# Encoder layer on one core: the long sequence's first phase with other rooms, earlier norms, a later fourth transposition and a held order

## The chip, the cores and the metric

One Trainium2 chip, one core of it. The metric is the device time of one execution in microseconds (us), median over the runs shown. The core's engines run beside each other and wait for each other through semaphores: TensorE (matmuls and transpositions), VectorE, ScalarE, GpSimd, and the queues that start DMA transfers (here mostly SyncE's, called the load queue below). Each engine takes its own instructions strictly in the order in which they stand in its stream.

## The reference

One hybrid encoder layer, run on two sequences with the same weights: the short one of 512 tokens (`x_sample`) and the long one of 1024 (`x_prompt`), model width 1024.

```python
def _trunk(x, ...):
    h = x
    h = h + _token_mixer(_rmsnorm(h, norm_mix_g), w_in, ...)
    h = h + jnp.square(jax.nn.relu(_rmsnorm(h, norm_mlp_g) @ w_mlp_up)) @ w_mlp_down
    return _rmsnorm(h, norm_final_g)

def _token_mixer(xn, w_in, ...):
    z = xn @ w_in
    qa, ka, va, qb, kb, vb, ga, gb = jnp.split(z, idx, axis=-1)
    qa = _apply_rope(_rmsnorm(qa per head, q_norm_g), cos, sin)
    ka = _apply_rope(_rmsnorm(ka per head, k_norm_g), cos, sin)
    o_a = _gqa_attention(qa, ka, va)
    o_b = _neighbourhood_attention(qb, kb, vb, rpb)
    merged = sigmoid(ga) * (o_a @ w_proj_a) + sigmoid(gb) * (o_b @ w_proj_b)
    return merged @ w_out
```

Branch A has 8 query heads in two groups, each with one key and one value head of 64. `_rmsnorm` divides by the root mean square of a row and multiplies by a gain.

## The kernel before

Every matmul of the mixer keeps about fp32 precision by splitting each operand into a high part (rounded by a ScalarE copy) and a low part (the difference, by VectorE), and by three products, high x high, high x low and low x high (`mm3`, L161 to L163). So each operand costs a ScalarE copy and a VectorE subtraction on its way to TensorE, for weights (`split`, L150 and L156) as for activations.

The two sequences run one after the other (`run`), then the MLP of both. Inside a sequence come the phases R (projections of branch A for one head group, twice), A (attention), B (neighbourhood attention) and G (gates, output projection, the norm for the MLP). Where the short sequence ends, its phase G already norms the first four 128-row tiles of the long one: for each of its own four tiles it loads a tile `xa` of the long sequence, norms it (`norm_tile`, tile `xnns`), and one tile later transposes it on TensorE and splits it into the long sequence's operands `xs_0h` and `xs_0l` (`p0_t` and `transpose_tile`, L241, L251, L255). `ahead` holds what waits to be transposed. The fourth is transposed after the loop.

The change lies in the long sequence's first phase R, group 0. Its loop goes over eight tiles `tt`. In each it:

- transposes tile `tt + 1` if phase G did not, and norms tile `tt + 2` (`p0`); tile 4 is normed at the end of `tt == 1` (`norm_to`, L232 and L234);
- loads the rotary rows `rt` (L537), and projects tile `tt` to queries, keys and the branch-A value (`zs`, 24 matmuls of 384 columns);
- from the third tile on, computes branch B's values of tile `tt - 2` (`values`: `zvs`, 24 matmuls of 256 columns, evicted to `vts`, L522 and L523) and transposes the normed heads of tile `tt - 2` (`heads_t`, L496 to L505);
- norms the heads of tile `tt`, the head norm below: five squares with sums on ScalarE (L561), one scaling on VectorE (`ms_As`, L144), a power of -1/2 on GpSimd (`rs_As`, L146), five products on VectorE (`ts`, L565), the value head's high copy and low part (`vhls`, L568 and L569), two products for the rotation on GpSimd (`us`, L577), then a product and a sum on VectorE (L583, `rrs` L585).

A tile norm of 1024 columns is a square with sum on ScalarE (L223 or L232), a scaling on VectorE, a power on GpSimd and a product on VectorE (L227 or L234). It is the same sequence as a head norm, with one row sum.

Order. The program is written in one order, and a planner at build time lays out each engine's stream: whatever its own timing says is ready, earliest in program order first. An instruction can therefore stand in the stream ahead of others that were written before it. `tc.keep_in_program_order(op)` pins an instruction behind the one that was written just before it on its engine. It adds no wait on the chip, it fixes the place in the stream. A run of instructions that are all pinned keeps exactly the written order; what isn't pinned may still come between them.

Rooms. A pool of a phase gives each tag (`xt`, `xn`, `rt`, `sq` and so on) its own rooms, side by side in the order in which the tags first ask. With `reuse_waits="tile"` a tile of a phase waits only for those tiles of the phase before that lay on the same bytes. Phase G's pool, from its bottom, in KB: 0 to 16 four rooms `k4` (loaded tiles `xa`, normed tiles `xnhs` and `xnns`), 16 to 28 six rooms for residual rows, 28 to 32 and 32 to 36 two gain rows, 36 to 52 two rooms of the output weights' second half. Phase R lies over it, before the change: loaded tiles `xt` 0 to 8, normed tiles `xn` 8 to 16, value weights 16 to 32, gain row 32 to 36, and from 36 on, over the output weights, `rt`, `sq`, `t`, `u`, `rr`, `vt`.

Accumulators are four banks tagged `mm` (projections and values) and two double banks tagged `big` (transpositions of tiles and heads). Longer-lived operands are in slots of 8 KB, six on the left, eleven on the right.

Of the kernel before, what the change touches and what calls it, by code (L numbers as in the profile page):

```python
# [18 lines left out]
P = 128  # L19
D = 1024  # L20
# [41 lines left out]
def encoder(ctx: ExitStack, tc: tile.TileContext, xs, outs, w):  # L62
# [79 lines left out]
    def rstd(ss, n, width, name):  # L142
        m = sml.tile([P, 8], F32, tag="ms", name=f"ms_{name}")
        nc.vector.tensor_scalar(m[:, :n], ss, 1.0 / width, EPS, op0=ALU.mult, op1=ALU.add)  # L144
# [27 lines left out]
    def load_cols(src, off, ncol, name, alloc=None, pin=False, hold=None):  # L172
# [9 lines left out]
        for k0 in range(0, nk, kp):  # L182
# [16 lines left out]
            cut = partial(split, hi[:, kk : kk + kn, :], lo[:, kk : kk + kn, :], rv)  # L199
# [30 lines left out]
    def norm_to(xn, src, gb, nm):  # L230
        ss = sml.tile([P, 8], F32, tag="ss", name=f"ss{nm}")
        nc.scalar.activation(xn, src, AF.Square, accum_out=ss[:, 0:1])  # L232
        r = rstd(ss[:, 0:1], 1, D, nm)
        nc.vector.scalar_tensor_tensor(xn, src, r[:, 0:1], gb, op0=ALU.mult, op1=ALU.mult)  # L234
        return xn
# [79 lines left out]
    class Trunk:  # L315
        def __init__(self, sq, x, t0):
# [5 lines left out]
            self.ready = 0  # L322

# [6 lines left out]
        def p0_t(self, tt, xn):  # L330
# [3 lines left out]
            transpose_tile(xn, self.xhl[tb], j, f"x{self.N}_{tt}", self.t0 + tt == 0)  # L334
            self.ready = tt + 1
# [7 lines left out]
    def run(tr, nxt, first):  # L343
# [88 lines left out]
        def load_v(g, alloc, pin=False):  # L432
            return load_cols(win, 1792 + 256 * g, 256, f"v{N}_{g}", alloc, pin)

        early = {}
        for g in range(2):
            with phase(f"phR{N}_{g}") as ph:
                xn_of = {}
                fresh = g == 0 and tr.ready < NT
                if fresh and not first:  # L440

                    xt = norm_load(x, tr.ready, ph, f"{N}_{tr.ready}")
# [46 lines left out]
                rr_of = {}  # L489

                def heads_t(tt):
# [8 lines left out]
                    nc.scalar.activation(kT[:, 0, ts_], pt[:, 2, :], AF.Copy)  # L500
                    for e in range(2):
                        nc.scalar.activation(qT[e][half[e], :, ts_], pt[half[e], 0:2, :], AF.Copy)
                    nc.vector.tensor_tensor(kT[:, 1, ts_], pt[:, 2, :], kT[:, 0, ts_].bitcast(F32), op=ALU.subtract)
                    for e in range(2):
                        nc.vector.tensor_tensor(  # L505
                            qT[e][half[1 - e], :, ts_],
                            pt[half[e], 0:2, :],
                            qT[e][half[e], :, ts_].bitcast(F32),
# [432 lines left out]
        with phase(f"phG{N}") as ph:  # L941
# [155 lines left out]
            while ahead:  # L1097
                nxt.p0_t(*ahead.pop(0))
# [548 lines left out]
```

## Time and profile before

| | |
|---|---|
| median of 3 runs | 2178.33 us (2174.81 to 2178.46) |
| the profiled execution | 2175.84 us |
| its span, first to last instruction | 2174.1 us |
| mean granted TensorE clock | 0.997 |
| TensorE busy / VectorE / ScalarE / GpSimd | 98% / 67% / 51% / 16% |

The long sequence's first phase begins at 394.8 us of the span, with the first projection, and its last head transposition is at 472.1. In the lines of a timeline the columns are start, duration, engine, source line, operation, the tile written and the tiles read, the shape, the count, and in brackets how long the engine had been idle and which instruction ended that. Consecutive records of one engine overlap a little, because instructions are pipelined: the distance from start to start is what an instruction costs its engine. A waits view names the engine and line that waited, the instruction that released it, the sum in us, how often, and the longest.

### The profile page before, as it was taken

To read this page: it belongs to the slowest core of one execution; us is meant where nothing else is said; L and a number is where in the kernel's file an instruction comes from. 1 tells how busy PE (TensorE), PEld (TensorE's weight loads), DVE (VectorE), ACT (ScalarE), POOL (GpSimd) and SP (SyncE) were. 2 spreads that over 40 slices of the span, in tenths; PEclk is the share of its full clock that TensorE was granted. 3 is DMA by queue.
4 is the path that set the end of the run, shared out by engine and by line. 5 is a ranking of instruction groups with operands and counts; after the bars stand their busy time and mean duration, and the time that the engine had idled before them with its cause. 6 is when DMAs were issued, how large, how long until landed. Compare 5 with 4: busy or idle time off the path is not lost. (4 is left out here: it accounts for less than half of the span.)

```text
span 2174.1 us, 32424 instructions
## 1 busy us (share of the span) xinstructions
PE 2133.4 (98%) x11180; PEld 1867.9 (86%) x11180; DVE 1456.2 (67%) x2835; ACT 1109.9 (51%) x2377; POOL 350.4 (16%) x458
## 2 busy tenths in 40 slices
PE   8999999899999999999999999999999999999998
PEld 8888778888898888888888899998999988888886
DVE  6665566767757754555772777778777777769663
ACT  5654553556645744545531466656555643433452
POOL 2232210333233223322300200003000000000000
PEclk9999999999999999999999999999999999999999
DMA  6436447620123133423463656568554799788561
GB/s 183 137 103 179 136 143 250 206 78 28 44 72 89 40 90 93 123 76 115 134 194 136 207 177 198 175 227 224 159 156 151 233 347 347 221 269 289 175 197 65
DMA packets 319917, 351.48 MB, mean 162 GB/s; under 512 B 31368, under 2 KB 255240, under 8 KB 319752
## 3 DMA queue, kind: packets, MB, share of 16 engines
q1 hardware_dynamic: 278071, 280.17, 41.3%
q10 hardware_dynamic: 36000, 52.18, 6.9%
q0 software_dynamic: 5680, 17.04, 2.8%
q8 instruction: 89, 1.46, 0.3%
q14 instruction: 77, 0.62, 0.1%
HBM read 265.37 MB, written 87.88 MB: 162 GB/s over the span
## 5 line engine op out<-in xcount | busy, mean ns | idle before, releaser
L163 PE MATMUL dn<-wd,al 128*128 128x512 f32 x624 | 242.8, 389 | 0.0
L162 PE MATMUL dn<-wd,ah 128*128 128x512 f32 x624 | 242.8, 389 | 0.0
L161 PE MATMUL dn<-wd,ah 128*128 128x512 f32 x624 | 242.7, 389 | 0.0
L1124 ACT ACTIVATE ah<-ar 128x512 fp32r<-128x512 f32 x168 | 104.0, 627 | 198.7 <-PE dn L162 179.6
L1125 DVE TENSOR_TENSOR al<-ar,ah 128x512 fp32r<-128x512 f32 x168 | 115.4, 695 | 73.4 <-ACT ah L1124 66.7
L162 PEld LDWEIGHTS dn<-wd,ah 128*128 128x128 f32 x624 | 117.1, 188 | 24.5
L161 PEld LDWEIGHTS dn<-wd,ah 128*128 128x128 f32 x624 | 117.1, 188 | 24.3
L163 PEld LDWEIGHTS dn<-wd,al 128*128 128x128 f32 x624 | 117.1, 188 | 24.2
L668 DVE TENSOR_TENSOR ptls<-pTs,pths 128x512 fp32r<-128x512 f32 x160 | 107.8, 687 | 37.4 <-ACT pths L667 36.7
L667 ACT ACTIVATE pths<-pTs 128x512 fp32r<-128x512 f32 x160 | 94.3, 598 | 75.1 <-PE pTs L662 72.8
L628 POOL TENSOR_SCALAR ps<-ps,rls 128x1024 f32<-128x1024 f32 (+1 forms) x96 | 96.9, 1010 | 217.3 <-DVE rls L627 197.2
L622 DVE TENSOR_REDUCE nms<-ss 128x1 f32<-128x1024 f32 (+1 forms) x96 | 99.9, 1041 | 25.7 <-PE ss L620 25.2
L161 PE MATMUL gpss<-xs_0h,w_gs 128*128 128x512 f32 x256 | 106.0, 414 | 0.8 <-DVE rlbs L838 0.7
L625 ACT ACTIVATE ps<-ss,nms 128x1024 f32<-128x1024 f32 (+1 forms) x96 | 93.3, 973 | 22.9 <-DVE nms L622 20.0
L662 PEld LDWEIGHTS pTs<-ident,ps 128*128 128x128 f32 x640 | 78.2, 140 | 27.9 <-POOL ps L628 3.9
L163 PE MATMUL gpss<-xs_0h,w_gs 128*128 128x512 f32 x256 | 101.5, 397 | 0.2 <-DVE w_gs L156 0.2
L162 PE MATMUL gpss<-xs_0l,w_gs 128*128 128x512 f32 x256 | 101.4, 396 | 0.0
L662 PE MATMUL pTs<-ident,ps 128*128 128x128 f32 x640 | 98.8, 274 | 1.1 <-DVE ptls L668 0.3
L146 POOL TENSOR_TENSOR rs_f<-ms_f,mhalf 128x1 f32<-128x1 f32 x6 | 4.0, 667 | 590.7 <-DVE ms_f L144 590.7
L1124 ACT ACTIVATE A<-S 128x512 fp32r<-128x512 f32 x128 | 75.8, 623 | 30.8 <-DVE S L1187 23.5
L831 DVE CUSTOM_DVE_ANT_0 sbss<-sbs,bms 128x384 f32<-128x384 f32 (+1 forms) x96 | 48.6, 508 | 58.9 <-issue 34.1
L161 PE MATMUL ud<-B,A 128*128 128x384 f32 x256 | 85.7, 335 | 1.5 <-DVE c L1242 1.5
(316 smaller groups left out, 6439.2 us busy)
## 6 DMA issues: line engine op xcount, KB each, us to landing
ar<-ud SPq DMA_DIRECT2D x120, 512.0 KB
br<-in_w_mlp_down_dram SPq DMA_DIRECT2D x72, 512.0 KB
rawu<-in_w_mlp_up_dram SPq DMA_DIRECT2D x64, 512.0 KB
ud<-c ACTq DMA_DIRECT2D x128, 192.0 KB
raw_gs<-in_w_in_dram SPq DMA_DIRECT2D x32, 512.0 KB
zgs<-sgs ACTq DMA_DIRECT2D x48, 256.0 KB
ud<-cs SPq DMA_DIRECT2D x64, 192.0 KB
raw_os<-in_w_out_dram SPq DMA_DIRECT2D x16, 512.0 KB
```

The source lines that it names most:

```text
L161: nc.tensor.matmul(out, ah, bh, start=start, stop=False, **kw)
L162: nc.tensor.matmul(out, ah, bl, start=False, stop=False, **kw)
L163: nc.tensor.matmul(out, al, bh, start=False, stop=stop, **kw)
L622: nc.vector.tensor_reduce(nm_, s, axis=AX.X, op=ALU.max, negate=True)
L625: nc.scalar.activation(p, s, AF.Exp, bias=nm_, accum_out=l)
L628: nc.gpsimd.tensor_scalar(p, p, rl, 1.0, op0=ALU.mult, op1=ALU.mult)
L662: nc.tensor.transpose(pt[:, j * P : (j + 1) * P], PP[u, j][:, kc * P : (kc + 1) * P], ident)
L667: nc.scalar.activation(hi, pt, AF.Copy)
L668: nc.vector.tensor_tensor(lo, pt, hi.bitcast(F32), op=ALU.subtract)
L831: nc.vector.tensor_tensor_reduce(out=sb, in0=so, in1=bm, op0=ALU.add, op1=ALU.min, scale=-1.0, scalar=3e38, accum_out=nm_)
L1124: nc.scalar.activation(hi, src, AF.Copy)
L1125: nc.vector.tensor_tensor(lo, src, hi.bitcast(F32), op=ALU.subtract)
```

## The change

Four edits, all in or for that phase; the short sequence's own first phase keeps its code.

1. Rooms. The tags of the head norm (`vt`, `sq`, `rt`, `t`, `u`, `rr`) ask for their first room before everything else, in that order, then the gain row, `xt`, `xn` and the value weights. They then lie at 0 to 16.25 KB, 16.25 to 20.25, 20.25 to 28.25, 28.25 to 36.25 and 36.25 to 52.25. The load of the gain row is written before the load of the fifth tile.
2. Norms a tile sooner. Tile 5 is normed at the end of `tt == 2`, tile `tt + 3` at the start of `tt` from 3 on, where it was tile `tt + 2`. Tile 4 stays at the end of `tt == 1`.
3. The fourth tile. Its norm in phase G goes to a left slot instead of a `k4` room. It is carried over, and its transposition is written behind the head norm of the first tile in phase R.
4. Order held. In this phase the tile norms, the splits of transposed tiles from the fourth on, and all ScalarE and VectorE instructions of values, head transpositions and head norms are pinned. The GpSimd instructions, the matmuls, the transfers and the splits of weights are not.

The new arguments `hold` and `pin_split` of the weight loads are not used by a call.

```diff
-    def rstd(ss, n, width, name):
+    def rstd(ss, n, width, name, pin=False):
         m = sml.tile([P, 8], F32, tag="ms", name=f"ms_{name}")
-        nc.vector.tensor_scalar(m[:, :n], ss, 1.0 / width, EPS, op0=ALU.mult, op1=ALU.add)
+        op = nc.vector.tensor_scalar(m[:, :n], ss, 1.0 / width, EPS, op0=ALU.mult, op1=ALU.add)
+        if pin:
+            tc.keep_in_program_order(op)
...
-    def norm_to(xn, src, gb, nm):
+    def norm_to(xn, src, gb, nm, pin=False):
         ss = sml.tile([P, 8], F32, tag="ss", name=f"ss{nm}")
-        nc.scalar.activation(xn, src, AF.Square, accum_out=ss[:, 0:1])
-        r = rstd(ss[:, 0:1], 1, D, nm)
-        nc.vector.scalar_tensor_tensor(xn, src, r[:, 0:1], gb, op0=ALU.mult, op1=ALU.mult)
+        op = nc.scalar.activation(xn, src, AF.Square, accum_out=ss[:, 0:1])
+        if pin:
+            tc.keep_in_program_order(op)
+        r = rstd(ss[:, 0:1], 1, D, nm, pin)
+        op = nc.vector.scalar_tensor_tensor(xn, src, r[:, 0:1], gb, op0=ALU.mult, op1=ALU.mult)
+        if pin:
+            tc.keep_in_program_order(op)
         return xn
...
-            transpose_tile(xn, self.xhl[tb], j, f"x{self.N}_{tt}", self.t0 + tt == 0)
-            self.ready = tt + 1
+            pin = self.t0 + tt == 0 or self.t0 > 0 and tt > 2
+            transpose_tile(xn, self.xhl[tb], j, f"x{self.N}_{tt}", pin)
+            self.ready = max(self.ready, tt + 1)
...
                 if fresh and not first:
 
+                    pre = {tag: shape(tag) for tag in ("vt", "sq", "rt", "t", "u", "rr")}
+                    gb = ph.tile([P, 1, D], F32, tag="gb", name=f"gb{N}", bufs=1)
+                    row_bcast(gb, w["norm_mix_g"], D)
+                    gb = gb[:, 0]
                     xt = norm_load(x, tr.ready, ph, f"{N}_{tr.ready}")
                     xn_next = ph.tile([P, D], F32, tag="xn", name=f"xn{N}_{tr.ready}", bufs=2)
                     room = [ph.tile([P, NC8, 256], F32R, tag="wv", name=f"wv{N}_{i}", bufs=2) for i in range(2)]
-                    gb = ph.tile([P, 1, D], F32, tag="gb", name=f"gb{N}", bufs=1)
-                    row_bcast(gb, w["norm_mix_g"], D)
-                    gb = gb[:, 0]
...
+                pin = fresh and not first
+
+                def K(op):
+                    if pin:
+                        tc.keep_in_program_order(op)
+
+                def next_norm(tt):
+                    xn = ph.tile([P, D], F32, tag="xn", name=f"xn{N}_{tt}", bufs=2)
+                    xn_of[tt] = norm_to(xn, norm_load(x, tt, ph, f"{N}_{tt}"), gb, f"{N}_{tt}", True)
...
-                    vt = ph.tile([P, 4, P], F32R, tag="vt", name=f"vt{nm}", bufs=2)
+                    vt = pre.pop("vt", None) or ph.tile([P, 4, P], F32R, tag="vt", name=f"vt{nm}", bufs=2)
                     zv4 = zv.rearrange("p (h d) -> p h d", d=HD)
-                    nc.scalar.activation(vt[:, :, 0:HD], zv4, AF.Copy)
-                    nc.vector.tensor_tensor(vt[:, :, HD:P], zv4, vt[:, :, 0:HD].bitcast(F32), op=ALU.subtract)
+                    K(nc.scalar.activation(vt[:, :, 0:HD], zv4, AF.Copy))
+                    K(nc.vector.tensor_tensor(vt[:, :, HD:P], zv4, vt[:, :, 0:HD].bitcast(F32), op=ALU.subtract))
...
                         tr.p0_t(tt + 1, xn_of.pop(tt + 1))
-                        if tt + 2 < NT:
+                        if first and tt + 2 < NT:
                             xn_of[tt + 2] = tr.p0(tt + 2, ph, gb, xt_of.get(tt + 2))
+                        elif tt + 3 < NT:
+                            next_norm(tt + 3)
...
-                    if fresh and not first and tt == 1:
-                        xn_of[tr.ready] = norm_to(xn_next, xt, gb, f"{N}_{tr.ready}")
+                    if fresh and not first:
+                        if tt == 0:
+                            tr.p0_t(*tr.carry.pop(0))
+                        if tt == 1:
+                            xn_of[tr.ready] = norm_to(xn_next, xt, gb, f"{N}_{tr.ready}", True)
+                        if tt == 2:
+                            next_norm(tr.ready + 1)
...
-                            ahead.append((tt, norm_tile(xt, gn, ph, f"n{nm}", "k4", 4)))
+                            if tt < NT - 1:
+                                ahead.append((tt, norm_tile(xt, gn, ph, f"n{nm}", "k4", 4)))
+                            else:
+                                xn = slot_left([P, D], F32, f"xnn{nm}")
+                                nxt.carry.append((tt, norm_to(xn, xt, gn, f"n{nm}")))
...
-            while ahead:
-                nxt.p0_t(*ahead.pop(0))
+            if nxt is not None:
+                nxt.ready = NT
```

The instructions of head transpositions (L500 to L505) and of head norms (L561 to L585) are wrapped in `K(...)` in the same way as those of `values`.

More of the change, by code (lines that the diff above doesn't have):

```diff
@@ L170, in encoder, with load_cols @@
     win = w["w_in"][0]
-    def load_cols(src, off, ncol, name, alloc=None, pin=False, hold=None):
+    def load_cols(src, off, ncol, name, alloc=None, pin=False, hold=None, pin_split=False):
         alloc = alloc or slot
@@ L198, in load_cols @@
                 kk = k0 % per
-            cut = partial(split, hi[:, kk : kk + kn, :], lo[:, kk : kk + kn, :], rv)
+            cut = partial(split, hi[:, kk : kk + kn, :], lo[:, kk : kk + kn, :], rv, pin_split)
             if hold is None:
@@ L322, in __init__ @@
             self.ready = 0
+            self.carry = []
         def p0(self, tt, pool, gb, xt=None):
@@ L430, in load_a, with load_v @@
             return wh, wl
-        def load_v(g, alloc, pin=False):
-            return load_cols(win, 1792 + 256 * g, 256, f"v{N}_{g}", alloc, pin)
+        def load_v(g, alloc, pin=False, hold=None):
+            return load_cols(win, 1792 + 256 * g, 256, f"v{N}_{g}", alloc, pin, hold, hold is not None)
         early = {}
@@ L556, in run @@
                         heads_t(tt - 2)
-                    sq = ph.tile([P, 5, HD], F32, tag="sq", name=f"sq{nm}", bufs=1)
+                    sq = pre.pop("sq", None) or ph.tile([P, 5, HD], F32, tag="sq", name=f"sq{nm}", bufs=1)
                     zq = z[:, :320].rearrange("p (h d) -> p h d", d=HD)
```

60 lines of the change are left out of this document (38 added, 22 removed).

## The prediction

> **What bounds the kernel now.** I read the page first, then the waits and the busy time by stretches around the change, then the timelines of TensorE, VectorE, ScalarE, GpSimd and of the load queue there.
>
> ```profile
> span 2174.1 us, 32424 instructions
> PE 2133.4 (98%) x11180; PEld 1867.9 (86%) x11180; DVE 1456.2 (67%) x2835; ACT 1109.9 (51%) x2377; POOL 350.4 (16%) x458
> ```
>
> TensorE is busy for all but 40.7 us. Nothing that the change touches removes a matmul, so it can only earn idle TensorE time. The next two views cover the place: busy time by stretch (TensorE, weight loads, VectorE, ScalarE, GpSimd, clock, DMA share, GB/s), and who TensorE waited for from 370 to 480 us.
>
> ```profile
> 410.00:420.00 10.00, 7.15 (x48) 6.51 (x48) 7.04 (x23) 7.38 (x42) 5.74 (x7) 1.00 0.70 226
> ...
> 450.00:480.00 30.00, 30.00 (x191) 27.43 (x190) 20.12 (x49) 15.51 (x50) 7.37 (x11) 1.00 0.33 100
> ...
> PE ptxs L241 <- DVE xns L227: 2.4, 2, 1.3
> PE zs L161 <- DVE vts L523: 1.7, 1, 1.7
> PE pqs L496 <- DVE rrs L585: 1.1, 1, 1.1
> PE zs L163 <- DVE xs_1l L255: 0.9, 1, 0.9
> PE ptxs L241 <- DVE ms_As L144: 0.5, 1, 0.5
> PE ptxs L241 <- DVE xnns L227: 0.4, 2, 0.2
> PE zs L162 <- DVE wgls L156: 0.4, 1, 0.4
> ```
>
> The waits add up to 7.4 us: that is all the change can earn, 0.34%. The clock is 1.00 and TensorE is full again from 450 on, so what is saved here shifts the rest. Every releaser is VectorE, which in the worst stretch is itself busy for 7 tenths only: its order and its waits matter, not its load.
>
> **Why VectorE is late.** ScalarE keeps its instructions in a fixed order, and there the first head norm stands behind the fourth tile's transposition and the value weights:
>
> ```profile
> 407.23 1.09 ACT L251 ACTIVATE xs_0h<-ptxs 128x512 fp32r<-128x512 f32 x2 [4.18 <-PE ptxs L241]
> 408.20 2.01 ACT L150 ACTIVATE wvs<-raw_vs 128x1024 fp32r<-128x1024 f32 x2
> 410.10 0.22 ACT L561 ACTIVATE sqs<-zs 128x64 f32<-128x64 f32 x1
> ...
> SPq L216 <- DVE xnns L227: 7.2, 1, 7.2
> ```
>
> ScalarE idles 4.18 us, then begins head norm 0 at 410.10. The load queue shows the other half: the fifth tile's load, on rooms of the four-KB tiles, waited 7.2 us for the fourth tile's norm, and the rotary rows stood behind it.
>
> **The change, step by step.** No instruction, byte or DMA is added or taken away; the terms are moves.
>
> Rooms. The value weights come to lie on the output weights (whose last matmul stands ahead of the first tile's projection), the first head norm's tiles on rooms that the third tile's transposition frees, the loads on rooms that the residual rows and the stage's last MLP norm free. The value weights can then be split before the head norm, and the rotary rows no longer queue behind the loads that waited. The norm-weight row (512 KB) is issued earlier, into a stretch of full DMA engines (share 1.06 from 396 to 398, 363 GB/s, row below): 512 KB at that rate is 1.4 us for whatever lands behind it. The bounds below hold that. The fourth tile's norm moves to a left slot, free after the last output matmul, so it costs nothing unless that norm were ready sooner.
>
> Head norm 0. On VectorE its first instruction is held behind the value weights' split, and the free work of the stage before stands there too:
>
> ```profile
> 396.00:398.00 2.00, 1.64 (x10) 1.32 (x9) 2.00 (x6) 0.00 (x0) 0.96 (x2) 1.00 1.06 363
> ...
> 398.51 1.28 DVE L227 SCALAR_TENSOR_TENSOR xnns<-xas,rs_ns,gns 128x1024 f32<-128x1024 f32 x1
> 403.18 1.28 DVE L255 TENSOR_TENSOR xs_0l<-ptxs,xs_0h 128x512 fp32r<-128x512 f32 x2
> 404.70 1.28 DVE L227 SCALAR_TENSOR_TENSOR xnns<-xas,rs_ns,gns 128x1024 f32<-128x1024 f32 x1 [0.24 <-POOL rs_ns L146]
> 409.56 2.49 DVE L156 TENSOR_TENSOR wvs<-raw_vs,wvs 128x512 fp32r<-128x512 f32 x4
> 411.96 0.16 DVE L144 TENSOR_SCALAR ms_As<-ssAs 128x5 f32<-128x5 f32 x1
> ```
>
> From 399.8 on that is 2 x 1.28 of these, one more 1.28 for the tile's other norm (as at 386.31 below), 2.49 for the value weights and 0.3 for small ones = 6.6, so the head norm starts at 406.4 if all of it goes first, at 405.1 if one 1.28 falls into its waits, at 403.8 if two do. I take 405.1, against 411.96 now: 6.9 us sooner.
>
> Order held. Now VectorE runs strictly in program order, and each wait inside a head norm stands open. Its length, from tile 6 (nothing but one short instruction between), a tile norm, a split of a transposed tile, and the evictions of values and heads:
>
> ```profile
> 452.72 0.17 DVE L144 TENSOR_SCALAR ms_As<-ssAs 128x5 f32<-128x5 f32 x1 [0.35 <-ACT sqs L561]
> 454.18 1.05 DVE L565 SCALAR_TENSOR_TENSOR ts<-zs,rs_As,gtab 128x64 f32<-128x64 f32 x5 [1.28 <-POOL rs_As L146]
> 456.51 0.49 DVE L583 TENSOR_TENSOR ts<-ts,rts 128x320 f32<-128x320 f32 x1 [0.76 <-POOL us L577]
> 456.92 0.42 DVE L523 TENSOR_TENSOR vts<-zvs,vts 128x256 fp32r<-128x256 f32 x1
> ...
> 385.47 0.15 DVE L144 TENSOR_SCALAR ms_hs<-sshs 128x1 f32<-128x1 f32 x1 [1.28 <-ACT xnhs L223]
> 386.31 1.28 DVE L227 SCALAR_TENSOR_TENSOR xnhs<-hs,rs_hs,gbms 128x1024 f32<-128x1024 f32 x1 [0.69 <-POOL rs_hs L146]
> 387.51 0.15 DVE L144 TENSOR_SCALAR ms_ns<-ssns 128x1 f32<-128x1 f32 x1
> ...
> 438.11 0.42 DVE L523 TENSOR_TENSOR vts<-zvs,vts 128x256 fp32r<-128x256 f32 x1
> 439.63 0.17 DVE L144 TENSOR_SCALAR ms_As<-ssAs 128x5 f32<-128x5 f32 x1
> ```
>
> Head norm: 452.72 to 456.92 is 4.2, and the sum of 0.4 behind it: 4.6. Tile norm: 385.47 to 387.51, 2.0. Split: 1.3. Evictions: 438.11 to 439.63, 1.5. Program order then gives, from the first mean to the fifth tile's split: 4.6 + 1.3 (tile 0, fourth tile's split), 4.6 + 2.0 (tile 1, norm), 1.5 + 4.6 + 2.0 (tile 2), 1.3: 21.9, so 427.0, its first half 426.3. A full tile is 4.6 + 2.0 + 1.3 + 1.5 = 9.4. TensorE's part of a tile:
>
> ```profile
> 446.25 1.06 PE L241 MATMUL ptxs<-ident,xns 128*128 128x128 f32 x8 [0.53 <-DVE ms_As L144]
> 447.07 0.42 PE L161 MATMUL zs<-wghs,xs_1h 128*128 128x384 f32 x1
> 451.35 0.28 PE L161 MATMUL zvs<-wvs,xs_1h 128*128 128x256 f32 x1
> 454.22 0.49 PE L496 MATMUL pqs<-ident,rrs 128*128 128x128 f32 x3
> 454.47 0.42 PE L161 MATMUL zs<-wghs,xs_1h 128*128 128x384 f32 x1
> ...
> 425.00 0.42 PE L161 MATMUL zs<-wghs,xs_1h 128*128 128x384 f32 x1
> ```
>
> Transposition 0.8, projection 4.3, values 2.9, heads 0.25: 8.2 from 446.25 to 454.47. So for the tiles that carry a norm VectorE sets the pace, not TensorE.
>
> Norms a tile sooner. The 2.4 and the 0.5 at the transpositions go, since each normed tile is ready 8 us ahead. The fourth tile's move takes the 1.7, the 1.1 and 0.2 away: sums and banks are then 5 us early.
>
> **The sum.** The fifth tile's projection begins at 425.00, after 1.7 + 1.1 + 0.4 + 0.2 of waits, so without them at 421.6. Its split is there at 426.3: 4.7 us late. The third tile's values (2.9, all inputs there) can run in that gap: I take it, since they are ready and next in order; 1.8 is left. The sixth and seventh tiles' projections each wait 9.4 - 8.2 = 1.2 more; the eighth's split comes without a norm (7.4 a tile) and isn't waited for. With the 0.4 and 0.2 left ahead of it: 0.6 + 1.8 + 2.4 = 4.8 instead of 7.4: a gain of 2.6. Bounds: 3.9 with the head norm at 403.8; with it at 406.4 and no values pulled ahead 0.6 + 6.0 + 2.4 = 9.0, a loss of 1.6. The profiled execution took 2175.84 (span and 1.7 around it), so 2173.2 for its like; the median of the runs shown lies 2.5 higher, so 2178.33 - 2.6 = **2175.7**.
>
> **The rivals.**
>
> B, all gaps filled. TensorE pulls the values of later tiles too, each 2.9 us and ready once its tile is split. Then only 0.6 and about 0.9 in front of the fifth tile stay: a gain of 5.9, **2172.4**. For it: two of the waits now are a transposition standing in the middle of a projection ahead of its data, which the earlier norms end. Against: four banks hold projections and values alike, and held order frees a value's bank only behind the norm.
>
> C, VectorE becomes the bound and the kernel is slower. The gate weights' splits are not held and are ready, so they drop into the opened waits and lengthen them:
>
> ```profile
> 412.27 1.18 POOL L146 TENSOR_TENSOR rs_As<-ms_As,mhalf 128x5 f32<-128x5 f32 x1 [7.60 <-DVE ms_As L144]
> 423.19 1.61 POOL L146 TENSOR_TENSOR rs_As<-ms_As,mhalf 128x5 f32<-128x5 f32 x1 [1.50 <-DVE ms_s L144]
> ...
> 423.08 0.68 DVE L156 TENSOR_TENSOR w_gs<-raw_gs,w_gs 128x512 fp32r<-128x512 f32 x1
> ...
> L156 DVE TENSOR_TENSOR w_gs<-raw_gs,w_gs 128x512 fp32r<-128x512 f32 x8 | 5.1, 683 | 0.0
> ```
>
> The power takes 1.18 alone and 1.61 beside such a split. Eight stand in this phase: 3.4 if all fall into waits, 5.1 if all fall between, 4.2 taken; with the bad bound of 1.6 that loses 5.8: **2184.1**. It decides where the chain, 405.1 + 47.5 for the first half of the eighth tile's split = 452.6, passes 454.47, where that tile's projection starts now: 1.9 us from my estimate. Against: six of the eight now come after 458.
>
> The Trainium skill speaks for C's mechanism: SBUF — State Buffer, "SBUF: two separate sides", has a VectorE instruction with two SBUF inputs and a GpSimd one that reads SBUF take a shared port pair in turn, the later one blocked for the other's whole length. By that rule a split may hold the power for its whole 0.68; the trace shows 0.43, and eight times 0.68 would be 5.4 instead of 3.4.
>
> D, the order that comes out is much as before, because most of it is bound by data: **2178.3**.
>
> **How the numbers follow.** A 0.40, B 0.28, C 0.21, D 0.11. A measurement of this kernel can tell about 0.2%, 4.4 us, from no change: faster is below 2174.0, slower above 2182.7. A's own range is 2174.4 to 2179.9, with 0.10 of its chance beyond on the fast side and 0.02 on the slow one; B counts as faster; C as slower but for 0.01; D gives 0.01 to each side. Faster 0.39, same 0.38, slower 0.23. The range 2171.0 to 2184.0 leaves about one in ten at each end.
>
> **What would show it.** Right: the first head norm's squares before 404, the values' split before them; no wait of a transposition for a tile norm; TensorE waiting for the low half of tiles 5 to 7 (the lines ending in xs_1l), near 4 us in all; VectorE idle for the power and the rotation in every head norm. Wrong, to the fast side: those low-half waits under 1.5 us. To the slow side: gate splits inside the head norms, powers near 1.6, the eighth tile's split after 454.5. A change of idle time after 480 would mean that the rest of the order moved, which none of this counts.

## The result and the profile after

| | median | lowest to highest | runs |
|---|---|---|---|
| kernel before | 2177.36 us | 2174.81 to 2178.46 | 6 |
| kernel after | 2183.92 us | 2180.66 to 2186.56 | 6 |

The changed kernel is slower: the ratio of the times is 1.0031, 95% interval 1.0022 to 1.0041, or 6.6 us. The time lies inside the range that was forecast, on the side that it called the less likely one. The profiled execution took 2180.66 us, the fastest of the six, so its trace shows 4.8 us of the loss (2180.66 - 2175.84).

The first lines of the page, after: busy time and its share of the span.

```profile
span 2178.9 us, 32420 instructions
PE 2136.9 (98%) x11180; PEld 1872.0 (86%) x11180; DVE 1458.1 (67%) x2835; ACT 1108.3 (51%) x2377; POOL 351.7 (16%) x458
```

The same 11180 matmuls took 3.5 us more of busy time, 2136.9 against 2133.4. With as many matmuls as before, that is slower matmuls. The rest is waiting.

Where it went is read from two marks in TensorE's timeline: the first matmul that waits for the low gate weights, near the phase's begin, and the first attention score, its end. Before:

```profile
397.77 0.44 PE L162 MATMUL zs<-wgls,xs_0h 128*128 128x384 f32 x1 [0.36 <-DVE wgls L156]
...
472.35 0.48 PE L619 MATMUL ss<-kTs,qTs 128*128 128x512 f32 x1
```

and after:

```profile
397.20 0.45 PE L164 MATMUL zs<-wgls,xs_0h 128*128 128x384 f32 x1 [0.35 <-DVE wgls L158]
...
476.80 0.47 PE L661 MATMUL ss<-kTs,qTs 128*128 128x512 f32 x1 [0.91 <-DVE qTs L535]
```

The phase between these marks was 74.6 us long and is 79.6 now. From the second mark to the last MLP matmul it is 1692.9 us before and 1693.2 after, so the whole loss was made inside the phase. Below, "the phase's length" is the distance of these two marks, and "after the begin" counts from the first, because the profiles of different kernels reach the phase up to 3.6 us apart. Of the 5.0 us that the phase grew by, about 3.3 are busy time and the rest waits, in this execution.

Who TensorE waited for from 370 to 480 us, after (line waited for, sum, times, longest):

```profile
PE zs L163 <- ACT xs_1h L257: 2.3, 1, 2.3
PE ptxs L247 <- DVE xs_1l L261: 2.1, 1, 2.1
PE ptxs L247 <- DVE xns L238: 2.1, 1, 2.1
PE zs L165 <- DVE xs_1l L261: 1.0, 1, 1.0
```

With 2.0 in five smaller lines this is 9.5 us where it was 7.4. The old waits for the values' eviction, for the head sum and for the sixth, seventh and eighth tile's norms are gone. In their place stand one for the fifth tile's norm (xns), one for the fifth tile's high half (xs_1h, at 427.58), one for the sixth tile's low half (at 439.79), one of the eighth tile's transposition for a double bank that the seventh tile's split frees late, and at the attention's begin the 0.91 of the row above. The eighth tile's, in TensorE's timeline:

```profile
449.92 1.06 PE L247 MATMUL ptxs<-ident,xns 128*128 128x128 f32 x8 [2.08 <-DVE xs_1l L261]
```

This transposition starts 52.7 us after the begin, and 48.5 in the kernel before (446.25): 4.2 of the 5.0 us are there by now.

VectorE's timeline, after, from the end of the stage before to the fifth tile's split (start, duration, then the columns as before):

```profile
400.50 0.15 DVE L144 TENSOR_SCALAR ms_hs<-sshs 128x1 f32<-128x1 f32 x1 [1.28 <-ACT xnhs L225]
401.34 1.28 DVE L229 SCALAR_TENSOR_TENSOR xnhs<-hs,rs_hs,gbms 128x1024 f32<-128x1024 f32 x1 [0.69 <-POOL rs_hs L148]
...
402.61 1.28 DVE L261 TENSOR_TENSOR xs_0l<-ptxs,xs_0h 128x512 fp32r<-128x512 f32 x2
404.13 1.28 DVE L238 SCALAR_TENSOR_TENSOR xnns<-xas,rs_ns,gns 128x1024 f32<-128x1024 f32 x1 [0.24 <-POOL rs_ns L148]
405.33 2.49 DVE L158 TENSOR_TENSOR wvs<-raw_vs,wvs 128x512 fp32r<-128x512 f32 x4
407.74 0.16 DVE L144 TENSOR_SCALAR ms_As<-ssAs 128x5 f32<-128x5 f32 x1
...
412.67 1.28 DVE L261 TENSOR_TENSOR xs_0l<-ptxs,xs_0h 128x512 fp32r<-128x512 f32 x2
413.87 0.16 DVE L144 TENSOR_SCALAR ms_As<-ssAs 128x5 f32<-128x5 f32 x1
...
418.60 0.15 DVE L144 TENSOR_SCALAR ms_s<-sss 128x1 f32<-128x1 f32 x1
419.42 1.28 DVE L238 SCALAR_TENSOR_TENSOR xns<-xts,rs_s,gbs 128x1024 f32<-128x1024 f32 x1 [0.67 <-POOL rs_s L148]
420.62 0.42 DVE L554 TENSOR_TENSOR vts<-zvs,vts 128x256 fp32r<-128x256 f32 x1
...
422.14 0.17 DVE L144 TENSOR_SCALAR ms_As<-ssAs 128x5 f32<-128x5 f32 x1
422.22 0.68 DVE L158 TENSOR_TENSOR w_gs<-raw_gs,w_gs 128x512 fp32r<-128x512 f32 x1
...
427.58 0.15 DVE L144 TENSOR_SCALAR ms_s<-sss 128x1 f32<-128x1 f32 x1
428.40 1.28 DVE L238 SCALAR_TENSOR_TENSOR xns<-xts,rs_s,gbs 128x1024 f32<-128x1024 f32 x1 [0.67 <-POOL rs_s L148]
429.60 1.28 DVE L261 TENSOR_TENSOR xs_1l<-ptxs,xs_1h 128x512 fp32r<-128x512 f32 x2
```

This is the held order at work. The fifth tile's norm (ms_s, xns) begins at 418.60, when the second head norm (413.87 to 418.60) is over to its last sum. Its product ends at 420.70, and the fifth tile's transposition starts at 420.85, after a wait of 2.06. In the kernel before nothing held that norm behind the head norm. It began 16.7 us after the begin there, and 21.4 here, and the transposition had nothing to wait for. VectorE's and TensorE's timelines, before:

```profile
414.51 0.15 DVE L144 TENSOR_SCALAR ms_s<-sss 128x1 f32<-128x1 f32 x1
...
419.97 1.03 PE L241 MATMUL ptxs<-ident,xns 128*128 128x128 f32 x8
```

Behind the fifth tile's norm, VectorE has the evictions, the third head norm and the sixth tile's norm, and only at 429.60 the subtraction of the fifth tile's split. ScalarE's half of that split is held too, and the longest wait, 2.25 us, is for it. ScalarE's timeline, after:

```profile
425.37 0.28 ACT L529 ACTIVATE kTs<-pqs 128x128 fp32r<-128x128 f32 x1 [4.52 <-PE pqs L525]
...
425.91 1.05 ACT L234 ACTIVATE xns<-xts 128x1024 f32<-128x1024 f32 x1
426.95 1.06 ACT L257 ACTIVATE xs_1h<-ptxs 128x512 fp32r<-128x512 f32 x2
```

The transposition was over by 422.3, but its copy (xs_1h) stands behind the third tile's value copy (425.81) and the sixth tile's square (425.91), and ScalarE was idle for 4.52 us before these.

### The profile page after: what moved, and what is told of

It reads as the page before. It is cut to its first block, busy times and chain, and to the rows that moved or that the text cites. A ratio compares the mean times of both kernels' runs of the same rounds, so it can differ in the third digit from the quotient of the medians.

```text
span 2178.9 us, 32420 instructions
## 1 busy us (share of the span) xinstructions
PE 2136.9 (98%) x11180; PEld 1872.0 (86%) x11180; DVE 1458.1 (67%) x2835; ACT 1108.3 (51%) x2377; POOL 351.7 (16%) x458
## 5 line engine op out<-in xcount | busy, mean ns | idle before, releaser
L667 ACT ACTIVATE ps<-ss,nms 128x1024 f32<-128x1024 f32 (+1 forms) x96 | 93.2, 971 | 23.0 <-DVE nms L664 18.8
L1171 DVE TENSOR_TENSOR A<-S,A 128x512 fp32r<-128x512 f32 x128 | 84.5, 686 | 4.4 <-ACT A L1170 4.3
```

The source lines that it names most:

```text
L667: nc.scalar.activation(p, s, AF.Exp, bias=nm_, accum_out=l)
L1171: nc.vector.tensor_tensor(lo, src, hi.bitcast(F32), op=ALU.subtract)
```

## The experiments

The expectations name theories by letters. H: the held order lengthens VectorE's chain and that is the loss. S is the rival to it, by which the order alone doesn't bring the loss. G: the gate-weight splits inside a held head norm (the mechanism of the prediction's rival C). W: VectorE's chain sets the pace whatever TensorE's clock. C, in the clock's experiment: the lower clock itself is the loss. All kernels were timed against the kernel before, whose median was 2176.9 to 2177.4 in the three sets of runs.

| kernel | median, us | ratio to before, 95% | phase, us | first head mean after the begin | lowest clock in 2 us |
|---|---|---|---|---|---|
| before | 2177.36 | | 74.6 | 14.2 | 1.00 |
| after | 2183.92 | 1.0022 to 1.0041 | 79.6 | 10.5 | 0.50 |
| e1, no order | 2173.15 | 0.9971 to 0.9989 | 70.9 | 10.5 | 1.00 |
| e2, no earlier norms | 2181.84 | 1.0013 to 1.0031 | 78.6 | 10.5 | 0.55 |
| e3, fourth tile as before | 2185.59 | 1.0023 to 1.0048 | 82.2 | 14.4 | 0.50 |
| e4, rooms as before | 2187.15 | 1.0029 to 1.0056 | 81.1 | 10.5 | 0.50 |
| e5, order alone | 2183.11 | 1.0019 to 1.0039 | 80.9 | 14.2 | 0.50 |
| e6, gate splits held | 2184.00 | 1.0019 to 1.0044 | 80.4 | 10.5 | 0.51 |
| e7, fillers | 2183.05 | 1.0018 to 1.0036 | 80.0 | 10.5 | 0.50 |
| e8, splits free | 2177.25 | 0.9995 to 1.0012 | 74.4 | 10.5 | 0.50 |
| e9, no order, no earlier norms | 2173.60 | 0.9980 to 0.9997 | 72.1 | 10.5 | 1.00 |
| e10, no order, fourth as before | 2176.23 | 0.9986 to 1.0004 | 73.5 | 14.2 | 1.00 |
| e11, no order, rooms as before | 2176.74 | 0.9988 to 1.0006 | 74.8 | 10.5 | 0.50 |

**e1, the three other parts without the held order.**

```diff
-            pin = self.t0 + tt == 0 or self.t0 > 0 and tt > 2
+            pin = self.t0 + tt == 0
...
-                pin = fresh and not first
+                pin = False
...
-                    xn_of[tt] = norm_to(xn, norm_load(x, tt, ph, f"{N}_{tt}"), gb, f"{N}_{tt}", True)
+                    xn_of[tt] = norm_to(xn, norm_load(x, tt, ph, f"{N}_{tt}"), gb, f"{N}_{tt}")
```

(and the same last argument where tile 4 is normed)

> The changed kernel with rooms, earlier norms and the later fourth transposition, but nothing pinned. Theory H (the held order leaves VectorE's waits inside the head norms open, so the fifth tile's low half comes at 430.9 instead of 428.2, TensorE then waits twice for over 2 us, and its clock is granted at about half for some 6 us): with the order free, splits and norms drop back into those waits, no wait of TensorE over 2 us, granted clock 1.00 in every 2 us from 416 to 446, first projection to first score 77 us or less (77.5 before, 82.6 with the change), total 2174 to 2178. Rival G (the gate weights' splits in the head norms' waits are what delays): they stay free to drop in, so the phase stays near 82 and the total near 2183. Rival R (the new rooms and the DMA order delay): stays near 2183 too.

It took 2173.15 us, a little below H's numbers, and beats both kernels. It keeps the rooms, and nothing holds the gate splits: G and R fall. Against the kernel before the ratio is 0.998, a gain of 4.2 us; the order undoes that and 6.6 us more, 10.8 in all. VectorE's timeline of this kernel shows what the planner does when it is free:

```profile
408.54 0.16 DVE L144 TENSOR_SCALAR ms_As<-ssAs 128x5 f32<-128x5 f32 x1
...
412.94 0.17 DVE L144 TENSOR_SCALAR ms_As<-ssAs 128x5 f32<-128x5 f32 x1
413.01 0.15 DVE L144 TENSOR_SCALAR ms_s<-sss 128x1 f32<-128x1 f32 x1
...
426.15 0.69 DVE L261 TENSOR_TENSOR xs_1l<-ptxs,xs_1h 128x512 fp32r<-128x512 f32 x1
427.15 0.69 DVE L261 TENSOR_TENSOR xs_1l<-ptxs,xs_1h 128x512 fp32r<-128x512 f32 x1
```

The second head norm and the fifth tile's norm begin in the same tenth of a microsecond, so their waits for GpSimd overlap. From the first mean to ms_s it is 4.5 us here and 10.9 after. The split comes as two halves, laid into the waits of other work. ScalarE's timeline shows the same of the squares. With the order, the second head's stand behind the first head's copy (vhls), for which ScalarE idles:

```profile
410.34 0.23 ACT L603 ACTIVATE vhls<-zs 128x64 fp32r<-128x64 f32 x1 [4.95 <-DVE ts L599]
...
411.41 0.24 ACT L594 ACTIVATE sqs<-zs 128x64 f32<-128x64 f32 x1
```

and in e1 they go ahead of it:

```profile
408.43 0.23 ACT L594 ACTIVATE sqs<-zs 128x64 f32<-128x64 f32 x1
...
411.14 0.23 ACT L603 ACTIVATE vhls<-zs 128x64 fp32r<-128x64 f32 x1 [0.54 <-DVE ts L599]
```

TensorE's waits in e1 add up to 4.0 us, the longest 1.75, and its clock stays at 1.00.

**e2, e3, e4: one part undone, the order kept.** e2 norms tile `tt + 2` again and tile 5 no sooner:

```diff
-                        elif tt + 3 < NT:
-                            next_norm(tt + 3)
+                        elif tt + 2 < NT:
+                            next_norm(tt + 2)
...
-                        if tt == 2:
-                            next_norm(tr.ready + 1)
```

> The changed kernel with the tile norms where they were (tile tt+2 behind the transposition at the start of tt), all else kept, order still held. Theory H: in the held order the fifth tile's norm of 2.0 us no longer stands ahead of that tile's fifth split, so the split ends 2.0 sooner, at about 428.9; the wait for it falls from 2.3 to under 1, the clock isn't halved behind it, and 2 to 4 us come back: total 2179 to 2182. The transpositions then wait for their norms again. Rival G: nothing but the transpositions' waits comes, total 2184 or more.

It took 2181.84 us, inside H's numbers, and its interval overlaps that of the changed kernel. Beside the fifth tile's 2.06, waits of 0.3 and 1.4 for later tiles' norms came back, as this line of its waits view shows, and still it is not slower than with the earlier norms:

```profile
PE ptxs L247 <- DVE xns L238: 3.8, 3, 2.1
```

The fifth tile's subtraction did begin 2.0 us sooner (30.4 after the begin, 32.4 in the changed kernel), but the wait for the high half stayed at 2.0 and the clock fell to 0.55 behind it, neither of which I had expected.

e3 writes the fourth tile's transposition back into phase G:

```diff
-                            if tt < NT - 1:
-                                ahead.append((tt, norm_tile(xt, gn, ph, f"n{nm}", "k4", 4)))
-                            else:
-                                xn = slot_left([P, D], F32, f"xnn{nm}")
-                                nxt.carry.append((tt, norm_to(xn, xt, gn, f"n{nm}")))
+                            ahead.append((tt, norm_tile(xt, gn, ph, f"n{nm}", "k4", 4)))
```

(and the transposition behind the loop instead of the one after the first head norm)

> The changed kernel with the fourth tile normed in its old room and transposed at the end of the stage before, all else kept, order held. Theory H: only the places of the fourth tile's split and of the first head norm are swapped in VectorE's order (1.3 against 4.6 us), the chain to the fifth tile's split keeps its length: 2182 to 2185, split still at 430 to 431.5. Rival F (the later fourth transposition delays the projections): 2178 or less.

The first mean came at 14.4 us after the begin, as in the kernel before, and the fifth tile's split at 435.63, later than I had expected; some 3 us of that lie ahead of the phase in this execution. The time is 2185.59, 0.6 above H's numbers; F falls.

e4 gives the tags their old places:

```diff
-                    pre = {tag: shape(tag) for tag in ("vt", "sq", "rt", "t", "u", "rr")}
-                    gb = ph.tile([P, 1, D], F32, tag="gb", name=f"gb{N}", bufs=1)
-                    row_bcast(gb, w["norm_mix_g"], D)
-                    gb = gb[:, 0]
                     xt = norm_load(x, tr.ready, ph, f"{N}_{tr.ready}")
...
+                    gb = ph.tile([P, 1, D], F32, tag="gb", name=f"gb{N}", bufs=1)
+                    row_bcast(gb, w["norm_mix_g"], D)
+                    gb = gb[:, 0]
```

> The changed kernel with the rooms asked for in the old order (and the gain row loaded behind the fifth tile as before), all else kept, order held. Theory H: the value weights' split waits for rooms freed at 403 to 406 and stands ahead of the first head norm, the loads wait for 406, so the head norm's start moves from 407.7 to 409 to 411 and the chain with it: 2184 to 2188. Rival R (the new rooms cost): 2180 or less.

2187.15 us, inside H's numbers, but not by the step that I had named: the first mean came no later (10.5 after the begin). The first head norm got longer, because GpSimd waited for the rotary rows, as its timeline shows:

```profile
415.62 1.16 POOL L613 TENSOR_TENSOR us<-ts,rts 128x160 f32<-128x160 f32 x2 [2.78 <-DMA rts<-in_rope_dram]
```

That is 4.3 us behind the first mean, and 2.8 in the changed kernel; the fifth tile's subtraction began 1.5 later after the begin. None of the three, taken away, removes the loss, and R falls. By the medians the held order costs 1.7 more without the fourth tile's move and 3.2 more without the rooms, but both intervals overlap that of the changed kernel.

**e5, the order alone,** on the kernel before: its `K(...)`, its pins in the tile norms and on the splits, nothing else.

```diff
-            transpose_tile(xn, self.xhl[tb], j, f"x{self.N}_{tt}", self.t0 + tt == 0)
+            pin = self.t0 + tt == 0 or self.t0 > 0 and tt > 2
+            transpose_tile(xn, self.xhl[tb], j, f"x{self.N}_{tt}", pin)
...
+                pin = fresh and not first
```

> The kernel before with the order of the phase held and nothing else: old rooms, old norms, fourth tile transposed at the end of the stage before. Theory H (the held order itself costs): slower than before by more than the whole change, since nothing starts the first head norm sooner: first mean on VectorE at 412 to 415, fifth split at 434 to 437, total 2184 to 2190. Rival S (the held order costs only where it meets the earlier norms or the later fourth tile): within 2 us of before, 2175 to 2180.

2183.11 us, a little below H's numbers, and far from a kernel that the order leaves alone. S falls: the order by itself makes the loss, here 6.2 us over the 2176.9 of the kernel before in the same runs. So under the held order the other three parts together earn nothing that can be measured (6.6 with them). The chain shows why. They start it 3.6 us sooner (10.5 after the begin, not 14.2), but from the first mean to the fifth tile's subtraction it is 18.8 us in e5 and 21.9 with them, since the fourth tile's split and the sixth tile's norm now stand in it. I had expected that subtraction at 434 to 437; it began at 430.98.

**e6, the two gate-weight splits** kept out of the third head norm, by pinning them behind the written order too.

```diff
-            nxt_w = load_cols(win, goff + c0 * P, P, f"g{N}_{goff}_{c0}")
+            nxt_w = load_cols(
+                win, goff + c0 * P, P, f"g{N}_{goff}_{c0}", pin_split=not first and (goff, c0) == (2304, 0)
+            )
```

> The changed kernel with the split of the first gate weight pinned where it is written (behind the seventh tile's head norm), so that it can't drop into the third tile's head norm. Theory H: only the 0.36 and 0.35 by which the power and the rotation of that head norm were stretched, and the 0.2 behind them, come back; the fifth split ends at 429.8 to 430.3 instead of 430.9, total 2181.5 to 2184. Rival G (the gate splits are what makes it slow): 2179 or less.

The third head norm went from 5.44 us (422.14 to 427.58 above) to 4.70, as VectorE's timeline of e6 shows:

```profile
424.45 0.17 DVE L144 TENSOR_SCALAR ms_As<-ssAs 128x5 f32<-128x5 f32 x1
...
429.15 0.14 DVE L144 TENSOR_SCALAR ms_s<-sss 128x1 f32<-128x1 f32 x1
```

So the splits did lengthen it, by 0.74, and the time did not move: 2184.00. The seventh tile's subtraction began 0.8 sooner after the begin, but at the attention's begin TensorE now waited 1.5. G falls here as well.

**e7, the clock.** The granted clock of the changed kernel, in stretches of 2 us (stretch, length, busy TensorE, weight loads, VectorE, ScalarE, GpSimd, then clock, DMA share, GB/s):

```profile
420.00:422.00 2.00, 1.15 (x9) 1.18 (x9) 1.97 (x5) 0.85 (x1) 0.00 (x0) 0.86 0.53 29
422.00:424.00 2.00, 2.00 (x12) 2.00 (x11) 0.91 (x4) 0.00 (x0) 1.54 (x1) 0.50 0.59 194
424.00:426.00 2.00, 1.33 (x8) 1.09 (x7) 1.61 (x6) 0.63 (x4) 0.91 (x1) 0.79 0.44 171
...
428.00:430.00 2.00, 2.00 (x13) 2.00 (x12) 1.60 (x2) 1.95 (x8) 0.37 (x1) 0.56 0.52 156
430.00:432.00 2.00, 2.00 (x10) 1.96 (x10) 1.33 (x4) 0.88 (x9) 0.56 (x1) 0.58 0.62 164
```

What these five stretches miss of the full clock is 2 x (0.14 + 0.50 + 0.21 + 0.44 + 0.42) = 3.4 us, about the 3.5 of extra busy time on the page. e7 puts 16 needless transpositions ahead of the fifth tile's and 18 behind the second tile's head transposition, into parts of the double banks that nothing reads, to keep TensorE busy there.

```diff
+        if keep is not None:
+            kf = keep.rearrange("p h d -> p (h d)")
+            for i in range(16):
+                nc.tensor.transpose(pt[:, i % 8 * P : (i % 8 + 1) * P], kf[:, i % 3 * P : (i % 3 + 1) * P], ident)
...
+                    if pin and tt == 1:
+                        for i in range(18):
+                            c = 512 + i % 4 * P
+                            nc.tensor.transpose(both[:, c : c + P], rrf[:, i % 3 * P : (i % 3 + 1) * P], ident)
```

> The changed kernel with 34 extra transpositions of the second tile's normed heads on TensorE, 16 ahead of the fifth tile's transposition and 18 behind the second tile's heads, written where nothing reads them; they fill two waits of over 2 us with work that waits for nothing else. Theory C (3.3 of the 5.0 us that the phase grew by are matmuls at half clock, granted 0.50 to 0.58, behind the two waits): the granted clock stays at 1.00 from 416 to 446, the low half still comes at 430 to 431.5, the phase shortens by 2 to 3 us, total 2179.5 to 2182. Rival W (the waits alone, the half clock runs inside time that VectorE sets anyway): 2183 to 2185.

2183.05 us, inside W's numbers. But the clock was moved, not kept: it stayed at 1.00 until 432 and fell behind a new wait of 2.8 us, at 433.88.

```profile
432.00:434.00 2.00, 0.12 (x1) 0.12 (x1) 2.00 (x3) 1.96 (x14) 0.00 (x0) 0.92 0.33 97
434.00:436.00 2.00, 2.00 (x8) 1.90 (x9) 1.33 (x3) 0.07 (x1) 0.56 (x1) 0.50 0.76 236
```

So no run of the held order kept the clock at 1.00 throughout. But e7 shows what the first of the two slow stretches was worth, since behind the fifth tile's transposition its clock was 1.00, and 0.50 in the changed kernel. From e7's timelines of VectorE and TensorE:

```profile
433.14 1.28 DVE L265 TENSOR_TENSOR xs_1l<-ptxs,xs_1h 128x512 fp32r<-128x512 f32 x2
...
453.49 1.06 PE L251 MATMUL ptxs<-ident,xns 128*128 128x128 f32 x8 [1.01 <-DVE xs_1l L265]
```

The fifth tile's subtraction begins 32.40 us after the begin (at 400.74), exactly as in the changed kernel (429.60), and the eighth tile's transposition 52.75 after it, where it was 52.72. So VectorE's chain had the same times in these two executions, whatever the clock did, and TensorE, sooner done, waited the longer: 2.80 for the low half. That speaks for W. So does the changed kernel's own trace: behind its slow stretches TensorE waits for VectorE again, 1.05 us at 439.79 and 2.08 at 449.92. For the second slow stretch, 428 to 432, this is read from the waits behind it; no run shows it alone.

**e8, the splits of the transposed tiles free,** everything else held.

```diff
-            pin = self.t0 + tt == 0 or self.t0 > 0 and tt > 2
+            pin = self.t0 + tt == 0
```

> The changed kernel with the splits of transposed tiles (copies and low parts of tiles 3 to 7) not pinned, everything else held. Theory H, sharpened: what costs is that these splits stand behind the whole head norm and tile norm; free, the fifth tile's low half drops into the third tile's head norm, ends by 427, TensorE has no wait of over 2 us, clock 1.00; total 2174 to 2179. If the other pins cost as much, it stays above 2181.

2177.25 us: of the 10.8 us that the order costs, 6.7 come back with this one pin, which holds both ScalarE's copies and VectorE's subtractions. The first copy of the fifth tile starts at 423.22, as soon as the transposition gives its half, and its projection at 426.52 waits for nothing. The subtraction's halves drop into the third head norm's waits again, though the fifth tile's norm stands behind the second head norm as after. VectorE's timeline of e8:

```profile
419.30 0.14 DVE L144 TENSOR_SCALAR ms_s<-sss 128x1 f32<-128x1 f32 x1
...
425.63 0.68 DVE L261 TENSOR_TENSOR xs_1l<-ptxs,xs_1h 128x512 fp32r<-128x512 f32 x1
...
427.41 0.68 DVE L261 TENSOR_TENSOR xs_1l<-ptxs,xs_1h 128x512 fp32r<-128x512 f32 x1
```

One wait of 2.2 us for that norm is left, and behind it the clock still halved (0.50 and 0.68 from 422 to 426), both against what I had expected. So a halved clock by itself doesn't cost the 6.6 us.

**e9, e10, e11: which part earns the 4.2 us of e1.** Each is e1 with one more part undone, by the diffs of e2, e3 and e4.

> Rooms and the later fourth transposition alone: norms as before, nothing pinned. If the norms a tile sooner carry the gain of the kernel without the order (2173.15), the transpositions wait for tile norms again as in the kernel before (2.4 + 0.5 us): 2175.5 to 2177.5, phase length 73 to 75 us. If rooms and the fourth tile carry it: 2172 to 2174.5, phase length 70.5 to 72.

2173.60 us. The waits for tile norms are back (2.1 us in two), and nothing that can be measured is lost: the earlier norms earn nothing.

> Rooms and earlier norms, nothing pinned; the fourth tile is transposed at the end of phase G as before. If the fourth tile's move carries the gain, ScalarE waits for that transposition again ahead of the first head norm, whose first mean comes after 411, and the later waits (1.7 and 1.1 before) return: 2175.5 to 2178, phase length 73 to 75.5. If not: 2172 to 2174.5, length 70.5 to 72.

2176.23 us, 3.1 more than e1. The first mean came at 14.2 us after the begin, and in TensorE's waits stand the 1.7 for the values' eviction and the 1.1 for the head sum again. So the fourth tile's move does what the prediction said it would, though not alone: the 1.1 is also there in e11, which keeps the move.

> Earlier norms and the later fourth transposition, nothing pinned; rooms as before. If the rooms carry the gain, the fifth tile's load and the rotary rows behind it wait for the fourth tile's norm again and the first mean comes 2 us or more later than in the kernel with rooms (10.5 us after the phase's start there): 2175.5 to 2178, phase length 73 to 75.5. If not: 2172 to 2174.5, length 70.5 to 72.

2176.74 us, 3.6 more than e1, but not by the step that I had named: the first mean came no later (10.5 us after the begin). The load queue shows the path. With the old rooms the fifth tile's load waits for the fourth tile's norm, and the rotary rows (L569) go out behind it. The queue's waits in e11:

```profile
SPq L218 <- DVE xnns L238: 7.2, 1, 7.2
```

In e11 that load is issued at 408.58 and the rotary rows from 409.50 on, in e1 at 399.86 and from 401.29. ScalarE then stood waiting for the tile, and GpSimd's rotation products for the first head norm came late:

```profile
413.96 1.06 ACT L234 ACTIVATE xns<-xts 128x1024 f32<-128x1024 f32 x1 [2.10 <-DMA xts<-in_x_prompt_dram]
```

```profile
415.49 1.16 POOL L613 TENSOR_TENSOR us<-ts,rts 128x160 f32<-128x160 f32 x2 [3.17 <-DVE vhls L604]
```

The value head's copy stands behind that square on ScalarE. The products started 4.7 us behind the first mean (410.83), in e1 2.8 behind it (408.54 to 411.33), and the second mean came at 16.8 us after the begin instead of 14.9. Whether they waited for the value head, as the row says, or for the rotary rows, as in e4, the records of e11 don't show. The size is less clear than the path: the profiled execution of e11 is the slowest of its 11 (2179.15, the fastest 2174.13), and its clock was at 0.50 to 0.74 from 430 to 438, which is 3.4 us. The mean clock of a whole run hints at how many had that: 0.995 in three of the 11, this one among them, and 0.997 or 0.998 in seven. The median of those seven is 2175.46, that of e1's nine such runs 2173.08. So some 2.4 of the 3.6 us are there without the lower clock.

## Why the prediction was wrong

The forecast was a gain of 2.6 us from an idle time of 7.4; it came out as a loss of 6.6.

**What failed: "With the 0.4 and 0.2 left ahead of it: 0.6 + 1.8 + 2.4 = 4.8 instead of 7.4".** This term prices the held order by the low halves of tiles 5 to 7 alone; whatever else the order makes late is put at nothing. TensorE's waits came to 9.5, and the low halves are only 1.05 of them. The rest of the excess lies in what the order holds besides:

- The fifth tile's norm, 2.06. "Norms a tile sooner. The 2.4 and the 0.5 at the transpositions go, since each normed tile is ready 8 us ahead" came true for the tiles that had these waits, the sixth to the eighth: none of them waits for its norm now. But the edit doesn't move the fifth tile's norm, and the order put it behind the second head norm. The prediction's own numbers hold 1.0 us of this wait: 405.1 + 4.6 + 1.3 + 4.6 + 2.0 is 417.6 for the normed tile, and the transposition at 419.97 less the 3.4 of waits ahead of it is 416.6.
- The copy on ScalarE, 2.25, where the sum had 1.8 for the low half. The sum follows VectorE's order alone, though ScalarE's is held as well.
- The double bank, 2.08. A split also frees the bank of its transposition, and the eighth tile's transposition waited for that.
- The attention's begin, 1.2.

Freeing the splits (e8) and freeing all (e1) bring back 6.7 and 10.8 us, and the order alone makes the loss on the old kernel (e5).

**The start of the chain was mis-sized.** "I take 405.1", with bounds of 403.8 and 406.4: it was 407.74, outside both, in an execution that reached the phase 0.6 us sooner. The rows above show all of the stage's free work ahead of the values' split. I had added its durations and none of the waits that stand inside it (1.28, 0.69 and 0.24 in the rows at 400.50, 401.34 and 404.13), although the prediction itself says that it is waits that make VectorE late. The move did make ScalarE's squares early, 404.27 where 404 was the mark.

**The chain's lengths were right.** Two head norms took 4.93 and 4.73 (4.6 predicted), a tile norm 2.02 (2.0), the evictions 1.52 (1.5), the split 1.2 (1.3). The third head norm took 5.44, because two gate splits fell into it. The sum is 23.1 instead of 21.9. Later splits began 9.45, 9.45 and 7.44 us apart (429.60, 439.05, 448.50, 455.94), for a predicted 9.4 and 7.4. The third tile's values were pulled into the gap ahead of the fifth tile's low half, as assumed: 14 of their 24 matmuls, from 428.04 to 430.85, at about half the clock. TensorE then didn't wait for that low half; the wait that counted stood ahead of these matmuls and was for the high half.

**Rival C** had the time, 2184.1, and the wrong mechanism. It needed eight gate splits to lengthen the head norms; two did, by 0.74 together, and holding these back earns nothing (e6). On its price the sentence from the Trainium skill held in direction (SBUF — State Buffer, "SBUF: two separate sides"): beside a split of 0.68 the power took 1.54 us, and 1.17 in e6 without it, so 0.37 more. That is less than the whole length of the split, but the split had begun first and had 0.51 left when the power began (422.39 to 422.90), which is nearer. That the measured time lies inside the range, 0.1 us below its end at 2184.0, is luck: neither the forecast's mechanism nor C's brought it there.

**Rival B**, all gaps filled, was 2172.4. That is what the change is worth when the order is left out (2173.15), though by other means: the longest waits that are left are for vhls, 1.75 us, and 4.0 us of waits stay in all.

**Not counted at all:** the clock. The prediction read 1.00 throughout the old trace and kept it. It lengthened the matmuls by 3.5 us, but, as e7 shows for the first slow stretch, that was time that TensorE would else have waited for VectorE.

## What to carry to other kernels

Holding an in-order engine to the written order turned every wait inside a chain into a wait of the engine, and what was queued behind it came late by the sum: before pinning, list who waits for each instruction that the pin puts last, on every engine that is pinned, the buffers that it frees included. Price a chain by its rows from start to start, waits and all, never by adding durations. And try the parts of a change apart: here two parts earn 4.2 us together and little that can be measured singly, one earns nothing, and the fourth takes back more than all of them.

## What the runs showed of the hardware

The clock halved behind some waits of about 2 us and not behind others. In the changed kernel it fell to 0.50 behind a wait of 2.06 and to 0.56 behind one of 2.25, in e8 behind one of 2.2; in the kernel before, e1, e9 and e10, with waits of 1.75 at most, it stayed at 1.00. Length alone doesn't decide: the 2.08 at 449.92 left it at 1.00, as one of 2.06 did in e2; a wait of 1.75 left it at 1.00 in e1, and in e11 it fell to 0.55 and 0.50 behind one of the same length (at 429.02) and one of 0.6 after it; and e5, where no single wait was over 1.9, had 0.67 and 0.50 from 416 to 420. The Trainium skill (TensorE: Matmul & The Clock Gate, "HAM oscillation — how this bites in real kernels") asks for no idle gaps of TensorE over about 3.4 us; here gaps of 1.75 to 2.25 were enough in some places. Its account of a free-running window (the same page, "Part 1: The HAM clock gate (the "warmup" mystery)") would allow one gap to halve the clock and an equal one not to, and one kernel to do so in some executions only; no run here tells that from other accounts.
